# Context transposes spread between the first gate blocks of the odd layer, and the third block put ahead of the first context blocks

## The chip, the core and the metric

The kernel runs on one core of a Trainium2 chip. TensorE (PE), VectorE (DVE), ScalarE (ACT), GpSimd (POOL) and the DMA queues, most of them fed by SyncE (SP), run side by side and meet at semaphores. The metric is the device time of one execution, in microseconds.

## The reference

One step of a small diffusion backbone with two layers, on 1024 latent tokens and 256 context tokens of width 1024. The even layer is a gated attention with two kinds of heads. The odd layer, in which the change lies, mixes the tokens by a Fourier transform:

```python
def odd_mix(h, w_in, w_out):
    u, gate = jnp.split(h @ w_in, 2, axis=-1)
    return (fourier_mix(u) * jax.nn.silu(gate)) @ w_out
```

Here `h` is the normalised input after shift and scale, once for the latent and once for the context rows, which are treated as separate sequences. `fourier_mix` is the real part of a two-dimensional FFT over the positions and over 256 channels of each of four groups. All of it is in float32. Outputs are the two normalised token arrays and the even layer's keys and values of the context.

## The kernel before, in words

All products are made from split numbers: each float32 operand becomes a high part (rounded) and a low part (the rest), and a product is three matmuls, high by high, high by low, low by high (`mm3`, line 265). The even layer is attention over 128-query blocks and fills the first 700 us or so. Its output projection (`out_proj`, accumulators named `oz`) takes the ten 128-row blocks of tokens in pairs; blocks 8 and 9 are the context and come last.

Each finished row block is squared and summed (L1344); each pair is normalised and folded into a sum and a difference (L1356 to L1358, `xo_`, `xe`), which makes even and odd parts for the Fourier transform. Four latent folds make the eight rows called quads. The quads are transposed on TensorE into PSUM (`quad_T`, L1274; banks `eoE0` to `eoE7` for the even part, `eoO0` to `eoO7` for the odd) and evacuated with shift and scale into the split tiles `EH["E"]` and `EH["O"]`. An evacuation with a shift (`eo_shifted`, L1256 to L1258) is two ACTIVATEs on ScalarE and a subtraction on VectorE, by way of a tile of the zone `h`; one without (`eo_scaled`, L1263 and L1264) is one ACTIVATE and one VectorE operation. The pair of the context goes the same way in `ctx_T` (L1293, banks `eoC0` to `eoC3`, tiles `EH["C"]`): each of its four calls makes four transposes into one bank, each followed by its evacuation. PSUM has three banks for transposes.

Then comes the gate. Its 1024 columns are eight column tiles, `ct` 0 to 7, and the weights `w_g1` are loaded 256 columns at a time, so that one load serves two tiles (`load_w`: four DMAs on SP's queue, L298, into raw tiles of zone `h`, and four splits, the high part by ScalarE, L277, the low part by GpSimd, L283). For each tile there is a main block for the latent rows, here m0 to m7: 24 matmuls of 512 columns from the even tiles (`g1E`) and 24 from the odd ones (`g1O`), evacuated by ScalarE and VectorE (L1473 to L1480), put through SiLU (L1453, L1454) and written to DRAM. And there is a context block, here p0 to p7: 24 matmuls of 256 columns (`g1c`). Between them stand eight steps (r0 to r7, `Rows.step`, L358 and L362) that sum up the rows of the adaptive-modulation weights for the layer's output gate on VectorE, each with a 512 KB load. After the gate comes the projection `u` with weights `wd`, the Fourier sums, and the output projection.

Memory in SBUF is handed out by hand from zones, in source order: `take` gives the buffer of a zone that was given back first, `drop` gives one back, and the new user waits for the last old one. `h` has nine buffers; the five zones in `BIG` have 43 together. PSUM accumulators of the gate come from a ring (`next_bank`) of four places: `g`, `s`, `a`, `s`, where `g` and `a` stand for one bank each and `s` for three.

The order of each engine's instructions is not the source's. A planner goes over the program when it is built: it takes, at each simulated time, the first in source order of the instructions that are ready by its own costs. So the source gives ranks and the order of buffers, and the planner fills gaps with what stands further down.

Of the kernel before, what the change touches and what calls it, by code (L numbers as in the profile page):

```python
# [59 lines left out]
AT_C, WO1 = (1, 1), ((0, 1, 2, 3), (), (4,), (5, 6), (7,))  # L60
PAIRS = ((0, 4), (2, 6), (3, 7), (1, 5), (8, 9))
FILL_C, NLATE = 2.9, 8
E_FQ, E_GD = "d", "d"
ORDER = "qa0 qa1 kb0 qb0 qb1 g0 g1 g2 g3"
FLATE = "f3"
# [74 lines left out]
def hybrid_step(ctx: ExitStack, tc: tile.TileContext, I, O):  # L140
# [40 lines left out]
    def next_bank(name):  # L181
        ring.rotate(-1)
        return bank(ring[-1], name)
# [102 lines left out]
    def load_w(src, width=256, tags="w", gap=None, lc=E_WL, each=None, later=None):  # L286
        out = []
        for kp in range(2):
            hi = take(tags, (P, 4, width), F32R)
            lo = take(tags, (P, 4, width), F32R)  # L290
            for j in range(2):
                r0 = (kp * 4 + j * 2) * P
                if width <= 256:
                    raw = take("h", (P, 2, width))
                else:
                    raw = take(("p", "pt", "q", "w"), (P, 2, width))
                if gap is None:
                    sp.dma_start(raw.a, src[r0 : r0 + 2 * P, :].rearrange("(j p) f -> p j f", p=P))  # L298
                else:
                    gap(raw, r0)  # L300
                if each is not None:
                    each(raw, kp * 4 + 2 * j)

                def fin(raw=raw, hi=hi[:, 2 * j : 2 * j + 2, :], lo=lo[:, 2 * j : 2 * j + 2, :]):
                    split(hi, lo, raw.a, XE["wh"], lc)
                    drop(raw)

                if later is None:
                    fin()
                else:  # L310
                    later.append(fin)
            out.append((hi, lo))
        return out
# [5 lines left out]
    def wk(w, k, c0, n):  # L319
        h, l = w[k // 4]  # L320
        return h[:, k % 4, c0 : c0 + n], l[:, k % 4, c0 : c0 + n]
# [962 lines left out]
    def ctx_T(rows, kq):  # L1284
        if kq == 0:
            EH["C"] = [(take(BIG, (P, 4, 256), F32R), take(BIG, (P, 4, 256), F32R)) for _ in range(2)]
        hh, hl = EH["C"][kq // 2]
        tp = t_bank(f"eoC{kq}")
        for j in range(2):
            k = 2 * kq + j  # L1290
            for n, row in enumerate(rows):
                c0 = j * 256 + n * P
                pe.transpose(tp[:, c0 : c0 + P], row[:, k * P : k * P + P], ident)  # L1293
                cols = slice(n * P, n * P + P)
                (eo_scaled if n else eo_shifted)(hh[:, k % 4, cols], hl[:, k % 4, cols], tp[:, c0 : c0 + P], k, 1)
        if kq == 3:
            drop(*rows)

    def eo_cols(key, k, c0, n):
        kper = 4 if key == "C" else 2  # L1300
        hh, hl = EH[key][k // kper]
        return hh[:, k % kper, c0 : c0 + n], hl[:, k % kper, c0 : c0 + n]

    gt0 = {}
    pairs = PAIRS
    kept = []
    half = {}
# [12 lines left out]
    def proj_step(i, j):  # L1320
        r = pairs[i][j]
        n = 2 * i + j
        v = r // 8
        if n == 4:
            for u in range(2):
                dve.tensor_scalar(mod2[:, :, u], modb[:, 1, :, u], (4.0, 2.0)[u], None, op0=ALU.mult)

        def between(h):
            for key, k in BETWEEN.get((n, h), ()):
                quad_T(key, k)  # L1330
            if (n, h) == (9, 1):
                for hw, lw in wout:
                    drop(hw, lw)
                for k in range(OPRE, 8):
                    quad_T("O", k)

        xr = out_proj("oz", r, ins.pop(r), wout, gt0[v], between)
        if n == 7:
            drop(gt0.pop(0))
        if r == 9:  # L1340
            drop(gt0.pop(1))
        yt = take("h", (P, D), BF16)
        sp.dma_start(x1d[r * P : (r + 1) * P, :], xr.a)
        act.activation(yt.a, xr.a, AF.Square, accum_out=ss1[:, r : r + 1])  # L1344
        drop(yt)
        kept.append(xr)
        if j == 0:
            return 0
        ssp = sm.tile([P, 4], F32, tag="ssq", name=f"ssp{i}")[:, 0:2]
        for jj, rr in enumerate(pairs[i]):  # L1350
            dve.tensor_copy(ssp[:, jj : jj + 1], ss1[:, rr : rr + 1])
        rs = rsqrt(f"r1{i}", ssp, 2, 1.0 / D, pw=PW1[i] == "1")
        xa, xb = kept
        kept.clear()
        xo_, xe = take(OB[0], (P, D)), take(OB[0], (P, D))
        act.activation(xo_.a, xb.a, AF.Copy, scale=rs[:, 1:2])  # L1356
        dve.scalar_tensor_tensor(out=xe.a, in0=xa.a, scalar=rs[:, 0:1], in1=xo_.a, op0=ALU.mult, op1=ALU.add)
        dve.scalar_tensor_tensor(out=xo_.a, in0=xa.a, scalar=rs[:, 0:1], in1=xo_.a, op0=ALU.mult, op1=ALU.subtract)  # L1358
        drop(xa, xb)
        if i == 4:  # L1360
            for kq in range(4):
                ctx_T((xe, xo_), kq)
            return 0
        half[pairs[i][0]] = xe, xo_
        if i % 2 == 0:
            return 0
        z = 0 in half
        (eh, oh), (el, ol) = half.pop(2 if z else 3), half.pop(0 if z else 1)
        ep = take(OB[0], (P, D))
        pick("fq", E_FQ).tensor_add(ep.a, el.a, eh.a)  # L1370
        pick("fq", E_FQ).tensor_sub(eh.a, el.a, eh.a)
        drop(el)
        op = take(OB[0], (P, D))
        pick("fq", E_FQ).tensor_add(op.a, ol.a, oh.a)
        if z:
            act.activation(op[0:1, :], oh[0:1, :], AF.Copy)
        pick("fq", E_FQ).tensor_sub(oh.a, ol.a, oh.a)
        if z:
            act.activation(oh[0:1, :], ol[0:1, :], AF.Copy)
        drop(ol)  # L1380
        quads[0 if z else 1] = (ep, eh, op, oh)
        return 0
# [61 lines left out]
    XE.update(XE3)  # L1444
    fl_.drain()

    wg = wgs[0]

    def silu4(d, n, scale):
        th = take(BIG, (P, n))
# [2 lines left out]
        drop(th)  # L1455

    r2 = Rows(1, 2, "ad12", BIG)
    for c in range(4):
        wn = load_w(I["w_g1"][:, 256 * c + 256 : 256 * c + 512], tags=BIG) if c < 3 else None
        todo = []  # L1460
        for c2 in range(2):
            ct = 2 * c + c2

            def main(ct=ct, c2=c2, wg=wg):
                ps = []
                for key in "EO":
                    ps.append(next_bank(f"g1{key}{ct}"))
                    mm3(ps[-1], [(*wk(wg, k, c2 * P, P), *eo_cols(key, k, 0, 512)) for k in range(8)])
                so = take("h", (P, 512))
                un = [take("h", (P, 512)) for _ in range(2)]  # L1470
                for e in range(2):
                    sl = so[:, e * 256 : e * 256 + 256]
                    act.activation(sl, ps[e][:, 256:512], AF.Copy)  # L1473
                    dve.tensor_add(un[e][:, 0:256], ps[e][:, 0:256], sl)
                    dve.tensor_sub(un[e][:, 256:512], ps[e][:, 0:256], sl)
                dve.tensor_scalar(un[1][:, 0:1], so[:, 256:257], 2.0, None, op0=ALU.mult)
                dve.tensor_scalar(un[1][:, 256:257], ps[1][:, 0:1], 2.0, None, op0=ALU.mult)
                d = take(BIG, (P, D))
                pick("gd", E_GD).tensor_add(d[:, 0:512], un[0].a, un[1].a)
                pick("gd", E_GD).tensor_sub(d[:, 512:1024], un[0].a, un[1].a)  # L1480
                drop(so, *un)
                silu4(d, D, 0.125)
                sp.dma_start(g1d[ct, :, 0:1024], d.a)
                drop(d)

            def part(ct=ct, c2=c2, wg=wg):
                ps = next_bank(f"g1c{ct}")[:, 0:256]
                mm3(ps, [(*wk(wg, k, c2 * P, P), *eo_cols("C", k, 0, 256)) for k in range(8)])
                so = take("h", (P, P))
                act.activation(so.a, ps[:, P:], AF.Copy)  # L1490
                d = take("h", (P, 256))
                dve.tensor_add(d[:, 0:P], ps[:, 0:P], so.a)
                dve.tensor_sub(d[:, P:], ps[:, 0:P], so.a)
                drop(so)
                silu4(d, 256, 0.25)
                sp.dma_start(g1d[ct, :, 1024:1280], d.a)
                drop(d)

            todo.append((main, part))
        todo[0][0]()  # L1500
        todo[1][0]()
        for k in ((), (0, 1, 2), (3, 4, 5), (6, 7))[c]:
            r2.step(k)
        todo[0][1]()
        todo[1][1]()
        drop_w(wg)
        wg = wn
    r2.finish("g")


# [457 lines left out]
```

## Time and profile before

| | us |
|---|---|
| median of 3 runs | 1191.62 |
| lowest and highest | 1185.96, 1196.26 |
| span of the profiled execution, first to last instruction | 1196.9 |

The page gives no other time for the profiled execution than its span. Over the span the granted TensorE clock was 0.990 of full speed on average. The DMA queues moved 168.81 MB, 141 GB/s on average. Lines of a timeline give start and duration in us, engine, line of the kernel, operation, output from inputs (zones or names of tiles, moving operand first for a matmul), shape, count, and in brackets the idle time before it with its releaser. Matmuls overlap in time, so that their pace is seen from start to start. Zones appear as names: `u`, `w`, `q`, `pt`, `p` and `h` are kinds of SBUF buffers.

### The profile page before, as it was taken

The numbers are of one execution on the slowest core, as the hardware profiler recorded it, in microseconds if no ns is written. First come the engines' busy times: TensorE is split into PE (matmuls) and PEld (weight loads), VectorE is DVE, ScalarE is ACT, GpSimd is POOL, SyncE is SP. The second block draws the span as 40 slices with busy tenths as digits, with TensorE's granted clock in tenths as the row PEclk, the third lists the DMA queues.
The fourth block names the chain that finished last, engine by engine and source line by source line (L and its number), as shares of the span: only waits on it lengthen the run. The fifth ranks groups of instructions, "written<-read, shape, count | busy, mean of one in ns | idle before, by whom it ended". The sixth has DMA issues, their size and how long they took to land.

```text
span 1196.9 us, 22002 instructions
## 1 busy us (share of the span) xinstructions
PE 1159.1 (97%) x8103; PEld 1037.9 (87%) x8103; DVE 834.5 (70%) x2006; ACT 577.1 (48%) x1159; POOL 286.0 (24%) x272
## 2 busy tenths in 40 slices
PE   8999999999999999999999989998999999999997
PEld 6788899999999998899888878886878888998886
DVE  2489778787777776678888867777755964367543
ACT  4442555555656655556676654532364225333211
POOL 2255644512222230011010035200212226200001
PEclk9999999999999999999999989998998999999999
DMA  9978512323532232444354477774214435364321
GB/s 327 365 257 272 160 59 69 89 77 113 148 89 78 76 95 84 100 120 116 83 148 105 131 223 203 232 224 160 85 45 136 147 115 167 109 186 150 141 105 54
DMA packets 130096, 168.81 MB, mean 141 GB/s; under 512 B 26298, under 2 KB 86454, under 8 KB 129988
## 3 DMA queue, kind: packets, MB, share of 16 engines
q1 hardware_dynamic: 127476, 158.74, 43.5%
q0 software_dynamic: 2368, 8.39, 2.3%
q8 instruction: 64, 1.05, 0.4%
q14 instruction: 44, 0.36, 0.1%
q10 hardware_dynamic: 144, 0.26, 0.1%
HBM read 123.19 MB, written 44.16 MB: 140 GB/s over the span
## 4 chain that ended last, share of the span: by engine, by line
PE 80%; DMA 9%; DVE 5%; ACT 2%; issue 2%; SPq 1%; POOL 1%; POOLq 0%; DVEq 0%; ACTq 0%
PE of L265 9%; PE q L265 8%; PE av L1051 8%; PE pt L1045 8%; PE ga L265 7%; PE sL L928 5%; PE u L265 5%; PE oz L265 4%; PE g1E L265 4%; PE g1O L265 4%; PE kv L265 3%; PE sC L928 2%; PE wa L559 2%; PE g1c L265 2%; DMA h<-i_w_out 2%
## 5 line engine op out<-in xcount | busy, mean ns | idle before, releaser
L277 ACT ACTIVATE pt<-pt 128x512 fp32r<-128x512 f32 (+1 forms) x265 | 146.8, 575 | 107.0 <-PE pt L1045 60.2
L1048 DVE TENSOR_TENSOR pt<-pt,pt 128x512 fp32r<-128x512 f32 (+1 forms) x264 | 170.8, 658 | 37.7 <-ACT pt L277 36.8
L1051 PE MATMUL av<-pt,u 128*128 128x256 f32 x1008 | 167.1, 289 | 0.7 <-ACT pt L277 0.7
L1045 PE MATMUL pt<-identr,p 128*128 128x128 f32 x1008 | 157.4, 273 | 1.1 <-ACT p L969 0.8
L265 PE MATMUL q<-w,u 128*128 128x256 f32 x960 | 143.9, 287 | 0.0
L1051 PEld LDWEIGHTS av<-pt,u 128*128 128x128 f32 x1008 | 138.9, 190 | 4.6 <-ACT pt L277 0.9
L265 PEld LDWEIGHTS q<-w,u 128*128 128x128 f32 x960 | 126.8, 188 | 4.9 <-issue 0.8
L1045 PEld LDWEIGHTS pt<-identr,p 128*128 128x128 f32 x1008 | 119.7, 141 | 8.0 <-ACT p L969 1.0
L969 ACT ACTIVATE p<-p,nm 128x1280 f32<-128x1280 f32 (+1 forms) x80 | 95.5, 1194 | 63.1 <-DVE p L962 62.8
L265 PE MATMUL ga<-u,w 128*128 128x512 f32 (+1 forms) x576 | 124.1, 360 | 0.8 <-DVE byp L1024 0.5
L265 PEld LDWEIGHTS ga<-u,w 128*128 128x128 f32 x576 | 93.6, 188 | 15.2 <-ACT pt L277 1.2
L283 POOL TENSOR_TENSOR w<-h,w 128x512 fp32r<-128x512 f32 x38 | 51.1, 1360 | 143.4 <-DVE w L279 115.0
L928 PE MATMUL sL<-u,q 128*128 128x512 f32 x256 | 82.4, 411 | 2.0 <-DMA q<-qd 2.0
L969 ACT ACTIVATE p<-p,NM 128x640 f32<-128x640 f32 (+2 forms) x80 | 59.2, 740 | 39.5 <-DVE p L962 39.4
L928 PE MATMUL sC<-u,q 128*128 128x256 f32 x320 | 61.8, 294 | 1.6 <-DMA q<-qd 1.0
L962 DVE TENSOR_SCALAR_CACHE_REDUCE p<-sL 128x512 f32<-128x512 f32 x64 | 43.9, 685 | 23.2 <-PE sL L928 14.2
L962 DVE TENSOR_SCALAR_CACHE_REDUCE p<-sL,nm 128x512 f32<-128x512 f32 x64 | 47.7, 745 | 13.7 <-PE sL L928 12.9
L265 PE MATMUL oz<-u,w 128*128 128x512 f32 x192 | 57.3, 403 | 0.0
L283 POOL TENSOR_TENSOR u<-h,u 128x512 fp32r<-128x512 f32 x16 | 20.6, 1293 | 138.0 <-ACT u L277 133.9
L928 PEld LDWEIGHTS sC<-u,q 128*128 128x128 f32 x320 | 48.8, 189 | 5.5 <-issue 1.1
L265 PE MATMUL oz<-u,u 128*128 128x512 f32 x160 | 48.7, 405 | 4.0 <-ACT u L277 2.5
L702 POOL TENSOR_TENSOR h<-h,rope 128x512 f32<-128x512 f32 (+1 forms) x18 | 21.9, 1214 | 126.4 <-ACT h L785 80.5
(728 smaller groups left out, 2569.8 us busy)
## 6 DMA issues: line engine op xcount, KB each, us to landing
q<-qd SPq DMA_DIRECT2D x80, 256.0 KB
h<-i_w_in SPq DMA_DIRECT2D x40, 256.0 KB
p<-i_ada_w SPq DMA_DIRECT2D x18, 512.0 KB
h<-i_w_out SPq DMA_DIRECT2D x32, 256.0 KB
pt<-i_ada_w SPq DMA_DIRECT2D x15, 512.0 KB
qd<-pt SPq DMA_DIRECT2D x20, 256.0 KB
q<-i_ada_w SPq DMA_DIRECT2D x9, 512.0 KB
qd<-q SPq DMA_DIRECT2D x18, 256.0 KB
```

What stands on the lines that cost most here:

```text
L265: pe.matmul(out, a, b, start=i == 0, stop=i == n - 1)
L277: act.activation(out, in_, AF.Copy)
L283: pick("lo" + lc, lc).tensor_sub(dst_l, src, dst_h)
L559: pe.matmul(acc[:, i * 256 : i * 256 + 256], wu[j][:, c0 : c0 + P], f[:, j, :], start=j == 0, stop=j == 1)
L702: pick("rope", XE["rope"]).tensor_mul(t1.rearrange("p t h (b c) -> p t (h b) c", b=2), y.rearrange("p t h (b c) -> p t (h b) c", b=2), cb)
L928: pe.matmul(ps, q_at(q, s, hc), keys, start=s == 0, stop=s == 1)
L962: dve.tensor_scalar(p[i][:, end[i] : end[i] + n], ps, sign, last[i], op0=ALU.mult, op1=ALU.min, accum_out=c)
L969: act.activation(p[i][:, 0 : end[i]], p[i][:, 0 : end[i]], AF.Exp, bias=last[i], scale=-1.0, accum_out=SU[:, t, hd + i, 0:1],)
L1045: pe.transpose(tp[:, jj * 256 + i * P : jj * 256 + i * P + P], p[i][:, off : off + P], ident)
L1048: dve.tensor_sub(pt[:, 1, 0:n], tp[:, 0:n], pt[:, 0, 0:n])
L1051: pe.matmul(acc, vv, pt[:, s, jj * 256 : jj * 256 + 256], start=c + jj + s == 0, stop=c + jj == nt - 1 and s == 1,)
```

## The change

The four `ctx_T` calls leave the end of the last projection step. That step now only keeps the two context rows in a list. The gate's main block makes one call after each of its two accumulations for the first two column tiles: the first after m0's even part, the second after m0's odd part, the third and the fourth after those of m1. The nested loop over weights and column tiles becomes a list of operations, in which l is a load of weights, m a main block, p a context block, r a step of `Rows`, and d the giving back of weights. In the same notation the order was and is:

```
before: l1 m0 m1 p0 p1 d0  l2 m2 m3 r0 r1 r2 p2 p3 d1  l3 m4 m5 r3 r4 r5 p4 p5 d2  m6 m7 r6 r7 p6 p7 d3
after:  l1 m0 m1 m2 p0 p1 d0  l2 r0 r1 r2 m3 p2 p3 d1  l3 r3 r4 r5 m4 m5 p4 p5 d2  r6 r7 m6 m7 p6 p7 d3
```

Thus m2 stands ahead of p0 and p1, and each group of r steps stands ahead of the main blocks that it followed. Before, all of `ctx_T` stood ahead of l1; now it stands behind it.

```diff
+G1 = "l1 m0 m1 m2 p0 p1 d0 l2 r0 r1 r2 m3 p2 p3 d1 l3 r3 r4 r5 m4 m5 p4 p5 d2 r6 r7 m6 m7 p6 p7 d3"
...
+    ctx_rows = []
...
         if i == 4:
-            for kq in range(4):
-                ctx_T((xe, xo_), kq)
+            ctx_rows.extend((xe, xo_))
             return 0
...
-    for c in range(4):
-        wn = load_w(I["w_g1"][:, 256 * c + 256 : 256 * c + 512], tags=BIG) if c < 3 else None
...
-        todo[0][0]()
-        todo[1][0]()
-        for k in ((), (0, 1, 2), (3, 4, 5), (6, 7))[c]:
-            r2.step(k)
-        todo[0][1]()
-        todo[1][1]()
-        drop_w(wg)
-        wg = wn
+    WG = {0: wgs[0]}
+
+    def g1_main(ct):
+        w, c2 = WG[ct // 2], ct % 2
+        ps = []
+        for n, key in enumerate("EO"):
+            ps.append(next_bank(f"g1{key}{ct}"))
+            mm3(ps[-1], [(*wk(w, k, c2 * P, P), *eo_cols(key, k, 0, 512)) for k in range(8)])
+            if 2 * ct + n < 4:
+                ctx_T(ctx_rows, 2 * ct + n)
...
+    for op in G1.split():
+        nm, i = op[0], int(op[1:])
+        if nm == "l":
+            WG[i] = load_w(I["w_g1"][:, 256 * i : 256 * i + 256], tags=BIG)
+        elif nm == "m":
+            g1_main(i)
+        elif nm == "p":
+            g1_part(i)
+        elif nm == "r":
+            r2.step(i)
+        else:
+            drop_w(WG.pop(i))
     r2.finish("g")
```

The evacuation, the SiLU and the write of a main block and the whole of a context block (`g1_part`) are as they were.

More of the change, by code (lines that the diff above doesn't have):

```diff
@@ L1445, in hybrid_step @@
     fl_.drain()
-    wg = wgs[0]
     def silu4(d, n, scale):
@@ L1457, in hybrid_step @@
     r2 = Rows(1, 2, "ad12", BIG)
-    for c in range(4):
-        wn = load_w(I["w_g1"][:, 256 * c + 256 : 256 * c + 512], tags=BIG) if c < 3 else None
[L1460 to L1499, printed above, removed]
-        todo[0][0]()
-        todo[1][0]()
-        for k in ((), (0, 1, 2), (3, 4, 5), (6, 7))[c]:
-            r2.step(k)
-        todo[0][1]()
-        todo[1][1]()
-        drop_w(wg)
-        wg = wn
@@ new lines, in hybrid_step @@
+    WG = {0: wgs[0]}
[7 more added lines that the diff above has]
+                ctx_T(ctx_rows, 2 * ct + n)
+        so = take("h", (P, 512))
+        un = [take("h", (P, 512)) for _ in range(2)]
+        for e in range(2):
+            sl = so[:, e * 256 : e * 256 + 256]
+            act.activation(sl, ps[e][:, 256:512], AF.Copy)
+            dve.tensor_add(un[e][:, 0:256], ps[e][:, 0:256], sl)
+            dve.tensor_sub(un[e][:, 256:512], ps[e][:, 0:256], sl)
+        dve.tensor_scalar(un[1][:, 0:1], so[:, 256:257], 2.0, None, op0=ALU.mult)
+        dve.tensor_scalar(un[1][:, 256:257], ps[1][:, 0:1], 2.0, None, op0=ALU.mult)
+        d = take(BIG, (P, D))
+        pick("gd", E_GD).tensor_add(d[:, 0:512], un[0].a, un[1].a)
+        pick("gd", E_GD).tensor_sub(d[:, 512:1024], un[0].a, un[1].a)
+        drop(so, *un)
+        silu4(d, D, 0.125)
+        sp.dma_start(g1d[ct, :, 0:1024], d.a)
+        drop(d)
@@ new lines, in g1_part @@
+    def g1_part(ct):
+        w, c2 = WG[ct // 2], ct % 2
+        ps = next_bank(f"g1c{ct}")[:, 0:256]
+        mm3(ps, [(*wk(w, k, c2 * P, P), *eo_cols("C", k, 0, 256)) for k in range(8)])
+        so = take("h", (P, P))
+        act.activation(so.a, ps[:, P:], AF.Copy)
+        d = take("h", (P, 256))
+        dve.tensor_add(d[:, 0:P], ps[:, 0:P], so.a)
+        dve.tensor_sub(d[:, P:], ps[:, 0:P], so.a)
+        drop(so)
+        silu4(d, 256, 0.25)
+        sp.dma_start(g1d[ct, :, 1024:1280], d.a)
+        drop(d)
```

## The prediction

> **What bounds the kernel now.** I read the page first, for the engine that carries the end.
>
> ```profile
> span 1196.9 us, 22002 instructions
> ...
> PE 1159.1 (97%) x8103; PEld 1037.9 (87%) x8103; DVE 834.5 (70%) x2006; ACT 577.1 (48%) x1159; POOL 286.0 (24%) x272
> ...
> PE 80%; DMA 9%; DVE 5%; ACT 2%; issue 2%; SPq 1%; POOL 1%; POOLq 0%; DVEq 0%; ACTq 0%
> ```
>
> TensorE is busy 97% of the span and carries 80% of the chain that ended last. So a change pays only where PE stands idle or runs slowly. The second view is busy time by stretches of time, cut around the stage that the change touches (columns: stretch and length, busy time and instructions of PE, PEld, DVE, ACT, POOL, granted clock, DMA share, GB/s).
>
> ```profile
> 838.00:894.95 56.95, 56.95 (x281) 46.51 (x280) 38.04 (x60) 28.52 (x53) 9.40 (x9) 1.00 0.18 62
> 894.95:906.77 11.82, 9.57 (x49) 8.23 (x48) 8.23 (x25) 8.91 (x24) 3.84 (x3) 0.71 0.19 59
> 906.77:1190.00 283.23, 283.23 (x1705) 245.19 (x1703) 165.72 (x329) 84.39 (x180) 54.04 (x52) 1.00 0.42 135
> ```
>
> PE has no idle time from 838 to 894.95 and none from 906.77 to the end, both at clock 1.00. Between them lies one bad stretch of 11.82 us: 2.25 us idle (11.82 - 9.57), clock 0.71. Nothing behind it can swallow a gain made there, because PE is full for the 283 us that follow; nothing behind it can add to one either. The third view is PE's order of instructions around that stretch.
>
> ```profile
> 894.72 0.39 PE L265 MATMUL g1O<-u,u 128*128 128x512 f32 x1
> 894.95 0.49 PE L1293 MATMUL eoC<-identr,u 128*128 128x128 f32 x3
> 896.29 0.38 PE L265 MATMUL g1c<-u,u 128*128 128x256 f32 x1 [0.85 <-ACT u L1263]
> 898.32 0.33 PE L1293 MATMUL eoC<-identr,u 128*128 128x128 f32 x1 [0.79 <-ACT h L1257]
> 899.01 0.47 PE L1293 MATMUL eoC<-identr,u 128*128 128x128 f32 x1 [0.37 <-ACT h L1257]
> 906.77 0.40 PE L265 MATMUL g1O<-p,u 128*128 128x512 f32 x1
> ```
>
> Main work (g1O) ends at 894.95; then PE has only context transposes (eoC) and context blocks (g1c) that need those transposes, and waits for ScalarE's evacuations. Main work resumes at 906.77. How much main work was done before the hole is the row of g1E alone: 48 matmuls, two blocks of 24, so m0 and m1.
>
> ```profile
> 866.00:895.00 29.00, 13.29 (x48) 8.43 (x48) 0.00 (x0) 0.00 (x0) 1.00 0.11 38
> ```
>
> The work at 906.77 is thus the third and fourth blocks. Why did it not come earlier? Its weights (l1) were late: SP's issues, SP's waits, and ScalarE's splits (L277) of those loads say so.
>
> ```profile
> 871.20 0.40 SPq L298 DMA_DIRECT2D h<-i_w_g  x1
> 892.35 0.38 SPq L298 DMA_DIRECT2D h<-i_w_g  x1
> 899.09 0.37 SPq L298 DMA_DIRECT2D h<-i_w_g  x1
> ...
> SPq L298 <- DVE u L1258: 26.8, 3, 20.7
> ...
> 874.74 0.63 ACT L277 ACTIVATE u<-h 128x512 fp32r<-128x512 f32 x1
> 895.35 0.63 ACT L277 ACTIVATE u<-h 128x512 fp32r<-128x512 f32 x1 [0.33 <-DMA h<-i_w_g]
> 901.72 0.63 ACT L277 ACTIVATE u<-h 128x512 fp32r<-128x512 f32 x1 [0.74 <-DMA h<-i_w_g]
> ```
>
> The first of l1's four loads is issued at 871.20 and split at 874.74. The others wait, 20.7 us the longest, for VectorE's L1258, the subtraction that ends the use of an `h` tile by a context transpose's evacuation. The last is split at 901.72. The nine `h` buffers are handed out in source order, and in the source the eight `h` tiles of the context transposes stand ahead of l1's raw tiles.
>
> **The change part by part.** *What can be won.* The stretch of 11.82 us holds this PE work:
>
> ```profile
> 894.95:906.77 11.82, 7.67 (x36) 7.14 (x36) 0.00 (x0) 0.00 (x0) 0.71 0.19 59
> 894.95:906.77 11.82, 3.27 (x11) 1.50 (x10) 1.82 (x6) 5.22 (x16) 0.71 0.19 59
> 930.63:936.29 5.66, 5.66 (x48) 5.61 (x47) 0.00 (x0) 0.28 (x1) 1.00 0.54 164
> ...
> 867.74 0.27 PE L1274 MATMUL eoE<-identr,p 128*128 128x128 f32 x1
> 867.85 0.27 PE L1274 MATMUL eoE<-identr,u 128*128 128x128 f32 x1
> ```
>
> The first row is g1c alone (36 matmuls), the second eoC alone (11 transposes), the third g1c alone where nothing disturbs it: 48 in 5.66 us, a pitch of 0.118 us. A transpose undisturbed has a pitch of 0.11 us (867.74 to 867.85). At full pace the stretch is 36 x 0.118 + 11 x 0.11 = 5.46 us, so it loses 11.82 - 5.46 = **6.36 us**. Its parts: 2.25 us idle; the clock; and 1.70 us left over, matmuls and transposes that come singly and are shown at their own length instead of their pitch. The clock part is seen in two stretches:
>
> ```profile
> 894.95:899.97 5.02, 2.77 (x13) 1.53 (x12) 2.43 (x8) 4.50 (x14) 2.56 (x2) 0.88 0.17 51
> 899.97:905.55 5.58, 5.58 (x27) 5.48 (x27) 4.85 (x16) 3.46 (x10) 1.28 (x1) 0.50 0.14 47
> ```
>
> In 5.58 us at clock 0.50 PE does 27 instructions (25 g1c, 2 eoC) that take 3.17 us at full pace: 2.41 us lost. No row gives the clock gate's rule, only that 2.77 us of work in 5.02 us was followed by half speed. The Trainium skill, "TensorE: Matmul & The Clock Gate", Part 1, puts the fall to half clock down to idle gaps of more than about 3 us, and its Part 4 adds that transposes do not count as PE work in the same way. The longest idle shown here is 0.85 us, so the trace differs from the first as stated and fits the second; by the gap rule alone the dip would not belong to this stall, and the sum would lose its 2.41 us.
>
> *Transposes spread, third main block ahead.* The number of matmuls and transposes is unchanged. What moves is source rank: l1's loads now stand ahead of all context evacuations, so their raw tiles follow the eoE evacuations and the last row's square; I expect all four issued and split before about 885 (issue to split took 3.5 us at 871.20, and nothing that they would follow is left after the last eoE evacuation). m2's two accumulations then stand ready when m1 ends. They cover the hole:
>
> ```profile
> 918.81 1.55 PE L265 MATMUL g1E<-w,u 128*128 128x512 f32 x6
> 920.20 1.09 PE L265 MATMUL g1E<-u,u 128*128 128x512 f32 x4
> ```
>
> Six matmuls in 920.20 - 918.81 = 1.39 us are 0.232 us each, so m2's 48 give 11.1 us of PE work, and the 16 transposes can be evacuated beside it and beside m0 and m1 instead of being waited for one by one. The context blocks p0 and p1 (5.66 us) then run where PE now runs m2. The cover's price if it fails is the hole as it is now.
>
> *A new order of waiting.* p0 and p1 are now behind m2 on PE; if l1 is late, 5.66 us of ready work waits behind m2, and with it the release of wg0 (d0) and l2's loads. Bank by bank nothing new is needed: m2's E bank is the one of m0's E, whose evacuation stood in the present order behind the same `h` tiles as l1 and moves forward with them. The two context rows stay in their buffers some 15 us longer, and the context tiles are taken after l1's; weights, E, O, context, accumulators and rows are 32 of 43 large buffers by the code, so nothing waits for one. I count all this at zero; the cover is m2's 11.1 us.
>
> *Row steps r0 to r2 ahead of m3 (and r3 to r7 likewise).* No step is added.
>
> ```profile
> 915.02 2.74 DVE L362 SCALAR_TENSOR_TENSOR u<-u,cs,u 128x512 f32<-128x512 f32 x4 [1.93 <-DMA u<-i_ada_w]
> ```
>
> Three steps are 3 x 2.74 = 8.2 us of VectorE ahead of m3's evacuation, and three 512 KB loads that SP issues earlier, behind l2's four, ahead of the blocks' output writes. The bank that m4's E needs is m3's E, free only once VectorE has read it; between the two PE has m3's O (5.6 us) and p2, p3 (5.7 us), 11.2 us against 8.2 and 1.9 of wait. Tight but covered: zero. Were it not, PE would wait for the difference.
>
> *The splits of l1 in the eoE/eoO evacuation.* This is the price. Three splits that now lie at 895 to 902 move to where ScalarE and VectorE feed PE's transposes: 3 x 0.63 = 1.9 us of ScalarE, each with a wait for its DMA (0.33 and 0.74 above; the longest near by is the first row here), and three subtractions on POOL.
>
> ```profile
> 908.61 0.63 ACT L277 ACTIVATE p<-h 128x512 fp32r<-128x512 f32 x1 [2.10 <-DMA h<-i_w_g]
> ...
> 873.62 1.28 DVE L1357 SCALAR_TENSOR_TENSOR u<-u,r14y,u 128x1024 f32<-128x1024 f32 x1 [0.66 <-ACT u L1356]
> 875.55 2.27 DVE L1358 SCALAR_TENSOR_TENSOR u<-u,r14y,u 128x1024 f32<-128x1024 f32 x1
> ...
> 875.45 1.29 POOL L283 TENSOR_TENSOR u<-h,u 128x512 fp32r<-128x512 f32 x1 [3.05 <-ACT u L277]
> ```
>
> While POOL made the one subtraction that is already there, a VectorE operation of the same size took 2.27 us and not 1.28: 0.99 us more. The Trainium skill, "SBUF — State Buffer", section "Who interferes with whom", states that a VectorE instruction with two SBUF inputs contends with a GpSimd instruction that reads SBUF; the trace agrees (2.27 against 1.28), and by that rule it speaks against this change, which moves three more such subtractions (up to 3.0 us of VectorE) there. From above, the cost is 3 x (0.63 + 2.10) = 8.2 us on ScalarE's queue, all of it reaching PE; from below it is zero, because the split at 874.74 with its subtraction cost PE nothing (no idle from 838 to 894.95). A gain is excluded: PE has no idle there. I take 0.3 us for each, 0.9 us, near the row of 874.74.
>
> *Sum.* -6.36 + 0.9 = -5.5 us. The page gives no time of the profiled execution besides its span: 1196.9 us, 0.6 above the slowest of the three runs (1196.26) and 5.3 above their median. The difference goes onto the median: 1191.6 - 5.5 = **1186 us** (1191.4 as a span). A measurement of this kernel can tell about 1% from no change, 12 us, and the whole hole is 6.4 us: 0.5%.
>
> **The rivals.**
>
> *The change doesn't do what it says.* The order on the engines isn't the source's: m3's O runs beside m2's O, and context matmuls run ahead of m2. A planner with costs of its own fills gaps; it can again release the context transposes as soon as a bank is free and leave PE with singles, or place l1 late. For it: in the present order it put them at 894.95 to 900 though they starved PE. Against it: it did so with no other main block ready. It gives back 0 to 2 us: 1190 to 1191.6.
>
> *Slower: a new hole in the transposes' stage.* Place: 866 to 890, ScalarE in order behind l1's DMA waits, VectorE stretched by POOL. Price: up to the 8.2 us above, plus a half-clock stretch of 2.4, less the 6.36 gained: +4.2, so 1196. It decides against the change once PE's new idle time passes about 4 us (4 + 2.4 = 6.4). That a hole of some us brings the clock down is seen twice, that 1.6 us did not, once:
>
> ```profile
> 690.00:700.00 10.00, 5.49 (x36) 4.94 (x35) 2.76 (x9) 3.35 (x9) 3.09 (x6) 0.87 0.73 241
> 730.00:740.00 10.00, 8.40 (x49) 7.18 (x48) 9.96 (x20) 4.36 (x11) 5.67 (x3) 1.00 0.35 119
> 810.00:820.00 10.00, 5.57 (x24) 3.94 (x23) 8.47 (x10) 3.02 (x6) 0.31 (x1) 0.84 0.60 174
> ```
>
> Against it: ScalarE has only 28.52 us of work in the 56.95 us before the hole, VectorE 38.04.
>
> *The half clock is not this hole's.* If the dip comes from something else and stays, the gain is 6.36 - 2.41 - 0.9 = 3.1 us: 1188.6. Against it: clock 1.00 in every stretch behind it, and 0.50 right after it.
>
> *The order elsewhere shifts.* A rebuilt plan may move things behind 907, where PE has nothing to gain, or ahead of 866, where 4.4 us (10 - 5.57) are idle in the stretch from 810 alone. No part of the diff points there; either sign, some us, 1180 to 1197.
>
> **How the numbers follow.** Forecast 0.54 (its own range 1182 to 1190: cost 0 to 3 us, and the runs' spread of 1185.96 to 1196.26 around a median of three); dip stays 0.04; no effect 0.20; new hole 0.12; order elsewhere 0.10. The range leaves out half of the last case and the far end of the slower one: 1180 to 1195. Faster by over 1% (below 1179.7) needs more than the hole holds, so it comes from the last case and the runs' spread: 0.08. Slower by over 1% (above 1203.5) needs a new hole worth more than priced: 0.06. Within 1%: 0.86.
>
> **What would show it.** Right: from 866 to the end PE without idle and at clock 1.00; 72 g1E matmuls ahead of the first g1c; eoC transposes apart from each other with main matmuls between; l1's four SP issues before 880. Wrong: idle time in eoE/eoO with a ScalarE or VectorE releaser; L277 waiting for `i_w_g` there; eoC still one by one with waits; PE waiting at m4 for a bank. The prediction fails as a whole if l1's loads stay behind another `h` user, or if what PE gains in this stage comes back as a new stop behind 907.

## The result: 0.5% slower, and the profile after

The changed kernel takes 1199.42 us against 1192.56 us before (medians of 17 runs each). The ratio is 1.0053, with a 95% interval of 1.0037 to 1.0068: 6.3 us slower (0.0053 x 1192.56), where 5.5 us faster was forecast. One run of the changed kernel took 2920.82 us and is left out of the ratio. The profiled execution of the changed kernel took 1196.54 us, its span is 1194.7.

The page of the changed kernel: span, busy time of PE, shares of the chain that ended last.

```profile
span 1194.7 us, 22000 instructions
...
PE 1158.0 (97%) x8103; PEld 1037.7 (87%) x8103; DVE 835.8 (70%) x2006; ACT 578.4 (48%) x1159; POOL 292.5 (24%) x272
...
PE 80%; DMA 9%; DVE 6%; issue 2%; ACT 2%; POOL 1%; SPq 1%; POOLq 0%; DVEq 0%; ACTq 0%
```

Nothing is to be seen at that scale, and this span is even shorter than the first one of before. The two executions differ most ahead of the change: the first gate product starts at 858.5 here and at 866.6 there. The 8 us are there before the change acts: up to l1's first load, at 853.20 here, every engine's instructions stand in the same order in both. So from here on I compare only the stretch from the first gate product (`g1E`) to the last product of the output projection (`of`), and call it **the stretch**. It took 329.1 us here and 323.2 in the profile of before. Busy time by stretches of time in the changed kernel (columns as in the prediction):

```profile
858.50:871.64 13.14, 11.65 (x63) 9.30 (x61) 9.73 (x15) 10.83 (x22) 6.75 (x5) 1.00 0.31 100
871.64:921.60 49.96, 49.32 (x267) 41.26 (x268) 29.75 (x63) 21.73 (x46) 8.10 (x4) 1.00 0.28 92
921.60:925.92 4.32, 0.52 (x5) 0.34 (x4) 3.28 (x8) 0.84 (x4) 0.00 (x0) 0.75 0.93 333
925.92:930.94 5.02, 5.02 (x24) 5.02 (x25) 5.02 (x14) 1.79 (x5) 0.00 (x0) 0.53 0.37 108
930.94:986.80 55.86, 55.86 (x290) 47.33 (x288) 39.84 (x75) 14.32 (x28) 14.30 (x10) 1.00 0.22 81
986.80:996.10 9.30, 7.37 (x76) 4.34 (x75) 3.00 (x4) 4.79 (x10) 6.81 (x6) 0.97 0.93 265
```

The old hole is gone: 49.96 us from 871.64 with 0.64 us idle and clock 1.00. In its place stand three new losses. PE's timeline names the releaser of each:

```profile
871.64 0.33 PE L1275 MATMUL eoO<-identr,pt 128*128 128x128 f32 x1 [1.49 <-DVE pt L1265]
...
925.92 5.18 PE L266 MATMUL g1c<-u,u 128*128 128x256 f32 x24 [3.80 <-DVE h L1491]
...
994.84 0.43 PE L1546 MATMUL xr<-q,e 128*32 128x130 f32 x8 [1.33 <-DMA q<-wd]
```

**The big one** is the second. PE waits 3.80 us for the bank of the context block that runs fourth (by the ring of banks it is p2, which takes p0's place); behind the wait 24 matmuls take 5.02 us at clock 0.53, where at the pitch of 0.118 us they take 24 x 0.118 = 2.83: 2.2 us more. ScalarE and VectorE in those microseconds:

```profile
921.75 0.75 ACT L1488 ACTIVATE h<-g1c 128x128 f32<-128x128 f32 x3 [1.04 <-PE g1c L266]
```

```profile
922.64 2.74 DVE L363 SCALAR_TENSOR_TENSOR u<-u,cs,u 128x512 f32<-128x512 f32 x4 [1.35 <-DMA u<-i_ada_w]
925.30 0.28 DVE L1490 TENSOR_TENSOR h<-g1c,h 128x128 f32<-128x128 f32 x1
925.50 0.28 DVE L1491 TENSOR_TENSOR h<-g1c,h 128x128 f32<-128x128 f32 x1
```

ScalarE has copied its half of the three context banks by 922.50. VectorE, which must read the other half (L1490, L1491) before a bank is free, stands at that time in a Rows step (L363; it is r1, since r0 ran at 903.69): first 1.35 us for the step's load, then 2.74 us for its four operations. The reads come after it, and PE goes on 0.14 us after the first L1491 has ended.

### The profile page after: what moved, and what is told of

Same layout as the page of the kernel before. It is cut to its first block, busy times and chain, and to the rows that moved or that the text cites. A ratio compares the mean times of both kernels' runs of the same rounds, so it can differ in the third digit from the quotient of the medians.

```text
span 1194.7 us, 22000 instructions
## 1 busy us (share of the span) xinstructions
PE 1158.0 (97%) x8103; PEld 1037.7 (87%) x8103; DVE 835.8 (70%) x2006; ACT 578.4 (48%) x1159; POOL 292.5 (24%) x272
## 4 chain that ended last, share of the span: by engine, by line
PE 80%; DMA 9%; DVE 6%; issue 2%; ACT 2%; POOL 1%; SPq 1%; POOLq 0%; DVEq 0%; ACTq 0%
PE of L266 9%; PE av L1052 9%; PE ga L266 8%; PE pt L1046 8%; PE q L266 8%; PE oz L266 5%; PE sL L929 5%; PE u L266 5%; PE g1O L266 4%; PE g1E L266 3%; PE kv L266 3%; PE sC L929 3%; PE g1c L266 2%; PE sB L1001 1%; DMA q<-qd 1%
## 5 line engine op out<-in xcount | busy, mean ns | idle before, releaser
L266 PE MATMUL of<-u,u 128*128 128x512 f32 (+1 forms) x187 | 58.0, 388 | 0.0
```

The source lines that it names most:

```text
L266: pe.matmul(out, a, b, start=i == 0, stop=i == n - 1)
```

## The experiments

Ratios are to the kernel before, those of the experiments with 12 runs each; b1 to b3 and a1 are one execution each and stand in the first two rows. The table has the stretch and its parts, in us; the gate is from the first `g1E` to the last `g1c`, the u stage from there to the first product of the Fourier sums. Idle time is that of PE. Each experiment has one profile, and four profiles of before differ by 2.0 us in the stretch: a smaller difference between two rows says something only where a named wait goes with it.

| kernel | gate | idle, clock | u stage | idle | stretch | ratio [95%] |
|---|---|---|---|---|---|---|
| before, four profiles | 125.4, 123.5, 124.9, 124.0 | 2.2, 2.6, 1.8, 1.9 | 69.6 to 69.7 | 0 | 323.2, 321.2, 322.7, 321.7 | 1 |
| after, two profiles | 128.2, 128.5 | 5.9 and 6.0, 0.97 | 72.6, 70.8 | 1.9, 1.6 | 329.1, 327.6 | 1.0053 [1.0037, 1.0068] |
| e1, steps back | 122.3 | 2.5, 1.00 | 70.6 | 0 | 321.2 | 0.9995 [0.9975, 1.0014] |
| e2, spread only | 125.5 | 4.3, 1.00 | 69.6 | 0 | 323.4 | 1.0024 [1.0001, 1.0047] |
| e3, m2 only | 122.7 | 1.9, 1.00 | 70.4 | 0 | 321.4 | 1.0001 [0.9980, 1.0023] |
| e4, steps only | 130.3 | 6.7, 0.97 | 69.4 | 0 | 327.8 | 1.0063 [1.0040, 1.0087] |
| f1, early loads | 123.7 | 3.1, 1.00 | 72.1 | 1.7 | 324.2 | 1.0016 [0.9991, 1.0041] |
| f2, r0 to r2 ahead | 128.3 | 6.0, 0.97 | 70.6 | 0 | 327.2 | 1.0045 [1.0025, 1.0065] |
| f3, r3 to r7 ahead | 122.3 | 2.6, 1.00 | 72.5 | 1.8 | 323.0 | 1.0011 [0.9992, 1.0031] |
| f4, l1's low parts on VectorE | 120.7 | 1.0, 1.00 | 70.6 | 0 | 319.6 | 0.9989 [0.9965, 1.0013] |
| h4, the same again | 120.9 | 1.0, 1.00 | 70.5 | 0 | 319.8 | 0.9995 [0.9975, 1.0015] |
| h1, bank by ScalarE | 122.3 | 2.3, 1.00 | 71.3 | 2.3 | 321.9 | 1.0014 [0.9994, 1.0034] |
| h2, m2 and l1 on VectorE | 124.9 | 2.8, 0.99 | 70.4 | 0 | 323.6 | 1.0028 [1.0007, 1.0048] |
| h3, all three | 120.8 | 0.7, 1.00 | 70.3 | 0 | 319.4 | 0.9997 [0.9980, 1.0015] |

### Which part of the change costs

The change has three parts: contexts spread, m2 ahead, r steps ahead. **e1** takes the steps back, **e2** and **e3** keep one of the other parts alone, **e4** keeps the steps alone (`early` stands for the four `ctx_T` calls put back at the end of the projection).

```diff
 # e1
-G1 = "l1 m0 m1 m2 p0 p1 d0 l2 r0 r1 r2 m3 p2 p3 d1 l3 r3 r4 r5 m4 m5 p4 p5 d2 r6 r7 m6 m7 p6 p7 d3"
+G1 = "l1 m0 m1 m2 p0 p1 d0 l2 m3 r0 r1 r2 p2 p3 d1 l3 m4 m5 r3 r4 r5 p4 p5 d2 m6 m7 r6 r7 p6 p7 d3"
 # e2: the order of before
+G1 = "l1 m0 m1 p0 p1 d0 l2 m2 m3 r0 r1 r2 p2 p3 d1 l3 m4 m5 r3 r4 r5 p4 p5 d2 m6 m7 r6 r7 p6 p7 d3"
 # e3: e1's order, early
 # e4: early, and
+G1 = "l1 m0 m1 p0 p1 d0 l2 r0 r1 r2 m2 m3 p2 p3 d1 l3 r3 r4 r5 m4 m5 p4 p5 d2 r6 r7 m6 m7 p6 p7 d3"
```

> The changed kernel with its r steps put back behind the main blocks (r0 to r2 behind m3, r3 to r5 behind m5, r6 and r7 behind m7); transposes spread and m2 ahead as in the change. Theory A (the r steps stand ahead of evacuations on VectorE, one of them waits for its load, and so a context block waits for its PSUM bank): the hole of 3.8 us at the context blocks and its half clock are gone, about 1191 to 1192, the 6.4 us of the old hole gained and some 1.5 us in the eoO stage and 3 us at the wd loads still lost. Theory B (the context blocks are bunched because the spread transposes finish late; the r steps are innocent): the hole stays, 1198 to 1200.

> The kernel before with one part of the change: the context transposes spread between m0 and m1; m2 stays behind the context blocks, the r steps where they were. Theory A: the old hole is filled because l1 comes early, no new one, about 1187 to 1189. Theory B: the late transposes leave PE waiting at the context blocks, 1192 or more. Both expect a VectorE wait of about 1.5 us in the eoO stage, where l1's low parts on GpSimd now run.

> The kernel before with one part of the change: m2 put ahead of p0 and p1; the transposes stay at the end of the last projection step. l1's raw tiles still follow the context evacuations in the h zone. If l1's lateness makes the old hole, it stays: 1191 to 1194. If only the rank of m2 behind the context blocks makes it, it is filled: 1186 to 1188.

> The kernel before with one part of the change: the r steps put ahead of the main blocks that they followed; transposes and m2 as before. Theory A: a new hole at m3 to m4 or at p2, p3, 1196 to 1200. Theory B: no new hole, 1191 to 1194.

With the steps back the loss is gone (0.9995); with the steps alone it is there in full (1.0063), in a kernel whose contexts are neither spread nor behind m2. PE's wait at the place of the hole, in e1 and then in e4:

```profile
927.12 3.06 PE L266 MATMUL g1c<-u,u 128*128 128x256 f32 x24 [0.57 <-DVE h L1491]
```

```profile
925.58 2.90 PE L266 MATMUL g1E<-w,u 128*128 128x512 f32 x6 [4.01 <-DVE h L1490]
```

3.80 us has become 0.57 in e1. In e4 it is 4.01, and the fourth block of even products waits there (72 `g1E` matmuls, three blocks, stand before it); by the ring it is m3's E, in p0's place. The victim changes, the releaser on VectorE is again a context block's read behind Rows steps.

Spread alone and m2 alone bring no gain that the times show: e3 stands at 1.0001, and e2 missed its gain of 2 to 4 us (1.0024, interval just above 1). In e2 l1 comes early and the planner runs m2 ahead of p0 and p1 by itself: 72 `g1E` and 96 `g1O` matmuls stand before 913.7. But m3's even products need p0's bank and wait 0.75 us for its read by VectorE (L1491), beside 1.0 and 0.8 us of waits for the context evacuations and 1.6 us at `eoO`: 4.3 us idle in all. In e3 the last of l1's splits still begins only at 901.34, and 1.9 us stay idle.

### Which steps, and is it their place on VectorE

**f2** and **f3** put one group of steps ahead each, on top of e1. **f1** leaves the change's order and issues the three loads of r0 to r2 right behind l1's.

```diff
 # f2
+G1 = "l1 m0 m1 m2 p0 p1 d0 l2 r0 r1 r2 m3 p2 p3 d1 l3 m4 m5 r3 r4 r5 p4 p5 d2 m6 m7 r6 r7 p6 p7 d3"
 # f3
+G1 = "l1 m0 m1 m2 p0 p1 d0 l2 m3 r0 r1 r2 p2 p3 d1 l3 r3 r4 r5 m4 m5 p4 p5 d2 r6 r7 m6 m7 p6 p7 d3"
 # f1
+G1 = "l1 w0 w1 w2 m0 m1 m2 p0 p1 d0 l2 r0 r1 r2 m3 p2 p3 d1 l3 r3 r4 r5 m4 m5 p4 p5 d2 r6 r7 m6 m7 p6 p7 d3"
+        elif nm == "w":
+            WT[i] = take(BIG, (P, D))
+            sp.dma_start(WT[i].a, ada_src(1, 2, i))
 ...
```

> The changed kernel with r3 to r7 put back behind their main blocks; r0 to r2 stay ahead of m3. If r0 to r2 alone make the hole of 3.8 us and its half clock, and r3 to r7 the loss of some 3 us at the wd loads: the hole stays and the wd stall goes, 1194 to 1196 against 1191 of before.

> The changed kernel with r0 to r2 put back behind m3; r3 to r7 stay ahead. By the same reading the hole at the context blocks goes and the wd stall (PE waits about 2 us for wd, then runs at a reduced clock) stays: 1193 to 1195. If r3 to r7 cost nothing: 1190 to 1191, as with all of them put back.

> The changed kernel, with the 512 KB loads of r0, r1 and r2 issued right behind l1 instead of in the steps themselves; the VectorE work of the three steps keeps its place in the list. Theory A1 (what hurts is that a step in VectorE's queue waits for a late load, with the evacuations behind it): the hole at the context blocks goes, about 5 to 6 us faster than the changed kernel, 1192 to 1194 against 1191 of before. Theory A2 (it is the 8.2 us of VectorE work ahead of the evacuations): the hole stays, 1197 or more.

The hole belongs to r0 to r2 and the stall in the u stage to r3 to r7. In f2 PE waits 3.85 us at the same place, and the u stage has no idle time; in f3 it is the other way round. Taken against e1 the two add up: 327.2 - 321.2 = 6.0 and 323.0 - 321.2 = 1.8 make 7.8, and the changed kernel stands 7.9 and 6.4 above e1 in its two profiles. The times show the first of the two costs (f2 1.0045) but not the second (f3 1.0011, interval from 0.9992).

Most of the 1.8 us goes with half clock. Behind the wait for `wd` the granted clock is 0.50 for about 3.4 us in f3 (994.4 to 997.8), f1 (from 993.2) and the first profile of the changed kernel (from 995.5), and their u stage takes 72.5, 72.1 and 72.6 us. In the second profile and in h1 the wait is shorter (0.86 and 0.83 us against 1.25 to 1.54) and the clock stays at 1.00: 70.8 and 71.3, against 70.6 in e1.

PE's timeline of f2:

```profile
929.46 5.28 PE L266 MATMUL g1c<-u,u 128*128 128x256 f32 x24 [3.85 <-DVE h L1491]
```

f1 did not test quite what it was made for. With the loads issued from 861.24 the planner also ran the steps themselves early: all twelve operations of r0 to r2 lie between 864.98 and 878.47, and the context blocks' reads come from 926.72 with no step just ahead of them (the step at 931.17 is r3). So it shows that the hole goes when no step stands ahead of the reads (PE waits 0.58), and says nothing of what an earlier load would do for a step that keeps its place on VectorE.

**h1** is the direct test: steps, order and loads as in the change, but a context block's bank is emptied by ScalarE alone, so that its release does not pass through VectorE.

```diff
-        so = take("h", (P, P))
-        act.activation(so.a, ps[:, P:], AF.Copy)
+        so = take("h", (P, 256))
+        act.activation(so.a, ps, AF.Copy)
         d = take("h", (P, 256))
-        dve.tensor_add(d[:, 0:P], ps[:, 0:P], so.a)
-        dve.tensor_sub(d[:, P:], ps[:, 0:P], so.a)
+        dve.tensor_add(d[:, 0:P], so[:, 0:P], so[:, P:])
+        dve.tensor_sub(d[:, P:], so[:, 0:P], so[:, P:])
```

> The changed kernel, with one edit: each context block's bank is emptied by ScalarE alone (it copies all 256 columns into SBUF, VectorE then adds and subtracts there), so that the bank's release no longer stands in VectorE's queue behind Rows steps; the steps stay where the change put them. Theory (the hole is the release stuck behind the steps on VectorE): the wait of 3.80 us before the fourth context block's products at 925.92 falls under 0.6, the half-clock stretch behind it goes (2.35 us), the gate's stretch is 122 to 123 against 128.2, and the time falls by about 5 us, ratio to before near 1.001; the wd stall of about 2 us in the u stage stays. Rival (the hole is the late transposes or the context blocks' place, and VectorE's queue only accompanies it): the hole and the low clock stay, 128 us, ratio 1.005.

VectorE's timeline of h1 at the same place (all times lie 8 us later in this execution), then PE's:

```profile
930.79 2.74 DVE L363 SCALAR_TENSOR_TENSOR u<-u,cs,u 128x512 f32<-128x512 f32 x4 [1.27 <-DMA u<-i_ada_w]
933.45 0.28 DVE L1490 TENSOR_TENSOR h<-h 128x128 f32<-128x128 f32 x1
```

```profile
929.83 3.67 PE L266 MATMUL g1c<-u,u 128*128 128x256 f32 x27
933.34 0.39 PE L266 MATMUL g1O<-p,w 128*128 128x512 f32 x1
```

VectorE does the same in the same order, with a wait of 1.27 us for the load (1.35 in the changed kernel) and the same step of 2.74 us ahead of the context blocks' additions. PE runs through it without a wait and at clock 1.00. The gate is 122.3 us, as in e1, and the ratio falls from 1.0053 to 1.0014. The stall in the u stage stays, as expected. So **the hole is shown to be the bank's release standing in VectorE's queue behind a step and its load**. Neither the late transposes nor the place of the context blocks makes it; both are as in the change here.

### The wait of eoO: GpSimd's subtractions

**f4** is e1 with the low parts of l1's weights made by VectorE instead of GpSimd; **h4** is the same kernel once more, **h2** makes this edit on e3, **h3** adds it and h1's edit to e1.

```diff
-            WG[i] = load_w(I["w_g1"][:, 256 * i : 256 * i + 256], tags=BIG)
+            WG[i] = load_w(I["w_g1"][:, 256 * i : 256 * i + 256], tags=BIG, lc="d" if i == 1 else E_WL)
```

> The changed kernel with all r steps put back behind the main blocks, and with the low parts of l1 subtracted on VectorE instead of GpSimd. If GpSimd's subtractions stretch VectorE's in the eoE stage and so make PE wait 1.5 us at eoO, the wait goes or shrinks to under 0.5 us and VectorE's operations there fall back to their usual 0.42 and 1.28 us: 1 to 1.5 us faster than with GpSimd, 1188 to 1189. If it is the work as such, VectorE has 2.7 us more of it and the wait grows: 1190 to 1192.

> The same kernel as f4_l1_low_dve, beside the others of this call: spread and third main block ahead, Rows steps as before, l1's low parts on VectorE. If its gain of 3.6 us in the profiled stage is real, the ratio is 0.997 (1188 to 1189 against 1191 to 1193); if the stage gain does not reach the end, 1.000.

> The third main block ahead of the first context blocks, transposes and Rows steps as before the change, and the low parts of l1's weights on VectorE rather than GpSimd. If the l1 splits' GpSimd work is what takes the 1.5 us wait of eoO for VectorE: that wait is gone, and the stretch from the first g1E to the end is 2 to 4 us under before's 323.2 (the m2-only kernel: 321.4), ratio 0.996 to 0.999. If the splits cost nothing that PE sees: as the m2-only kernel, ratio 1.000.

> Transposes spread and the third main block ahead, as in the change; Rows steps as before it; l1's low parts on VectorE; context banks emptied by ScalarE alone. If every hole found is a release in VectorE's queue: no wait over 0.6 us of PE in the gate, clock 1.00, the gate 119.5 to 120.7 against 125.4 before, ratio 0.995 to 0.998. If the bank's release no longer matters once the steps are back: as the kernel without this last edit, gate 120.7, ratio 0.999.

VectorE in the changed kernel while GpSimd subtracts, GpSimd there (e1 has the same picture), then VectorE in f4:

```profile
867.56 2.19 DVE L1360 SCALAR_TENSOR_TENSOR u<-u,r14y,u 128x1024 f32<-128x1024 f32 x1
869.67 1.52 DVE L1259 TENSOR_TENSOR pt<-h,u 128x256 fp32r<-128x256 f32 x1
```

```profile
866.70 4.21 POOL L284 TENSOR_TENSOR u<-h,u 128x512 fp32r<-128x512 f32 x2 [0.26 <-ACT u L278]
```

```profile
869.92 0.68 DVE L284 TENSOR_TENSOR u<-h,u 128x512 fp32r<-128x512 f32 x1
870.52 1.28 DVE L1360 SCALAR_TENSOR_TENSOR u<-u,r14y,u 128x1024 f32<-128x1024 f32 x1
871.72 0.42 DVE L1259 TENSOR_TENSOR pt<-h,u 128x256 fp32r<-128x256 f32 x1
```

Two VectorE operations lose 0.91 and 1.10 us beside GpSimd. Without it they take 1.28 and 0.42, and the subtraction that VectorE does in GpSimd's stead costs 0.68. The wait of 1.49 us before `eoO` is gone, the gate falls by 1.6 us (122.3 to 120.7; 120.9 in h4). h2 missed: where the contexts are not spread, l1's splits do not lie there. It has three of them from 892.32 on, in the old hole, so nothing was to be won there, and more is lost in the old hole than in e3 (2.8 us idle against 1.9, clock 0.99, gate 124.9). Its ratio of 1.0028 lies above 1, more than its stretch explains. That also shows what moves l1: with the contexts spread, its first split in e1, e2 and the changed kernel begins at 856.94 to 861.79 and its last at 867.78 to 872.67; without, in e3 and h2, the last begins at 901.34 and 898.86.

The gate of h3 as one row, then that of e1:

```profile
863.50:984.30 120.80, 120.11 (x645) 101.11 (x644) 87.15 (x174) 50.49 (x104) 21.28 (x16) 1.00 0.32 105
```

```profile
863.40:985.70 122.30, 119.78 (x645) 100.95 (x643) 86.39 (x171) 49.75 (x104) 26.44 (x20) 1.00 0.31 104
```

h3 has 0.69 us without a matmul (120.80 - 120.11), no wait over 0.5 us, and the shortest stretch of all. Its expected ratio of 0.995 to 0.998 was missed all the same. No version is measurably faster than before; f4, h4 and h3 stand at 0.9989, 0.9995 and 0.9997, so that of h4's two expectations "does not reach the end" came out.

### Is the old hole's half clock there every time

> The kernel before, unchanged: a second profile of it. The first one holds 323.2 us from the first gate product to the last output product, with 2.24 us without a matmul and 2.41 us of half clock in the hole at 894.95 to 906.77. If the half clock belongs to every execution: 323 us again, granted clock 0.97 in the gate's stretch. If it comes and goes: 320.5 to 321.5 us, the idle time in place, clock 0.99 to 1.00, and the gain that a filled hole can bring is that much smaller.

> As the run before it, a third profile of the kernel before: 323 us with a clock of 0.97 in the gate's stretch if the half clock is of every execution, 320.5 to 321.5 us with 0.99 to 1.00 if it isn't.

> A fourth profile of the kernel before, read as the two ahead of it: 323 us and 0.97, or 320.5 to 321.5 us and 0.99 to 1.00.

> The changed kernel, unchanged: a second profile of it. If its own hole (3.80 us of waiting and 2.35 us of half clock behind it) belongs to every execution: 328 to 330 us from the first gate product to the last output product, clock 0.97. If the half clock comes and goes here too: about 326.5 us with the wait in place.

The 11.82 us of the old hole, in the three new profiles of before, at the same distance from the first `g1E`; then the gate of the changed kernel in its second profile:

```profile
889.45:901.27 11.82, 9.79 (x60) 7.92 (x59) 8.68 (x25) 8.77 (x24) 3.86 (x3) 1.00 0.22 72
```

```profile
885.95:897.77 11.82, 10.01 (x51) 8.58 (x50) 8.76 (x25) 8.85 (x24) 3.83 (x3) 0.71 0.20 66
```

```profile
890.75:902.57 11.82, 9.88 (x55) 8.29 (x54) 8.71 (x25) 8.85 (x24) 3.83 (x3) 0.86 0.20 68
```

```profile
857.10:985.60 128.50, 122.51 (x645) 103.45 (x643) 86.52 (x171) 49.53 (x103) 28.30 (x19) 0.97 0.28 97
```

The idle time is there each time (2.03, 1.81 and 1.94 us, against 2.25 in the first). The half clock comes and goes: clock 0.71 in the first profile, then 1.00, 0.71 and 0.86, with 49, 60, 51 and 55 instructions done in the same 11.82 us. The stretch of before is 322.2 us on the mean of four, not 323.2. The changed kernel's hole has both times the wait of 3.8 us and the half clock. On the means, 328.35 - 322.2 = 6.15 us, which is what the times say (6.3).

## Why the prediction was wrong, point by point

**The step that failed** is "Row steps r0 to r2 ahead of m3 (and r3 to r7 likewise) ... Tight but covered: zero." It priced one bank, that of m4's E. It did not ask which other reads stand behind the steps on VectorE at the time when the planner lets them run: those of the three context blocks that ran first, whose banks the next blocks need. m2 put ahead of p0 and p1 brought the context blocks to just that place, but e4 shows that the steps hit a bank without that too. Measured: 6.0 us for r0 to r2 (f2 against e1: 3.85 us of waiting where e1 has 0.57, and the half clock behind it), 1.8 us for r3 to r7 (f3 against e1, most of it a half clock that not every execution has). Its own fallback, "Were it not, PE would wait for the difference", was the right mechanism at another bank; and it left out the half clock behind the wait.

**"Nothing behind it can swallow a gain made there ... nothing behind it can add to one either"** failed with it. A stage in which PE has no idle time is full in the old order; a change of order makes its own holes in it. The prediction's last line named this outcome, "a new stop behind 907", but gave it no price.

**The old hole, -6.36 us.** That it could be filled, and by what, was right: idle 0.64 us from 871.64 to 921.60. The size was too large. f4 and h4, where the new waits are away, have a stretch of 319.6 and 319.8 against 322.2: 2.5 us won. In the gate alone it is 3.65 us (120.8 against 124.45 on the means); 0.9 us of it goes again in the u stage (70.55 against 69.65), without idle time there, and why stays open. Of the prediction's terms, the 2.41 us of half clock were those of one execution; of four profiles of before one has none of it.

**The rule on the clock.** The prediction noted that the half clock came with a longest idle gap of 0.85 us. Both kinds of hole are now in the rows: 3.80, 3.78, 3.85 and 4.01 us of waiting (after twice, f2, e4) each went with a clock of 0.97 in the gate; 0.85 us and less did in some executions of before and not in others, before the `xr` products, which need `wd`, 1.25, 1.33 and 1.54 us did (f3, after, f1) while 0.83 and 0.86 did not (h1, after again), and 1.49 to 1.64 us at `eoO` never did.

The Trainium skill, "TensorE: Matmul & The Clock Gate", section "What's actually happening", says that activity is judged over a free-running window of about 3.4 us. The traces agree: in all 18 the granted clock holds for whole multiples of 3.41 us ahead of its last record, and half clock lasted 3.41 or 6.83 us each time, but for the spell that the end of the span cuts off (in the changed kernel it is 0.50 from 923.8 to 930.6 and 1.00 on both sides). This raster lies differently against the stage in each execution: in the four of before an edge comes 28.8, 27.9, 28.4 and 29.4 us behind the first `g1E`, where the old hole begins at 28.35, and the hole had 6.83, 0, 6.83 and 3.41 us of half clock. That the place of the raster decides it is likely but not shown, and neither is how little work in a window brings the clock down.

**l1's loads ahead** was right. SP's issues in the changed kernel, then the last of ScalarE's splits of l1:

```profile
853.20 0.38 SPq L299 DMA_DIRECT2D h<-i_w_g  x1
...
860.88 3.96 SPq L299 DMA_DIRECT2D h<-i_w_g  x3
```

```profile
867.78 0.63 ACT L278 ACTIVATE u<-h 128x512 fp32r<-128x512 f32 x1
```

All four are issued by 864.84 and split by 868.41, where before the last split began at 901.72.

**The splits' price, 0.9 us**, had the right mechanism and was too low: PE waits 1.49 us, and taking GpSimd out of it gives 1.5 us (321.2 to 319.7 on the mean of f4 and h4). It went by the one split that had cost nothing; three together did not fit under the same cover. The Trainium skill, "SBUF — State Buffer", section "Who interferes with whom", says that a VectorE instruction with two SBUF inputs contends with a GpSimd instruction that reads SBUF. It is borne out by f4: 2.19 and 1.52 us become 1.28 and 0.42.

**The sum of the measured terms**: -2.5 + 1.5 + 6.0 + 1.8 = +6.8 us, against +6.9 and +5.4 in the stretch of the two profiles (the second has no half clock in the u stage) and +6.3 in the times. The prediction took 1% for the least that a measurement can tell; here 0.5% came out clear of its interval.

**The rivals.** The slower one came nearest in price (+4.2 us) and had the shape (over 4 us of new idle time and a half-clock stretch), but the wrong place and mechanism, so that its nearness is luck: it put the hole into the transposes' stage at 866 to 890, where 1.49 us were lost; the 3.80 us came at 922, at a bank. "What would show it" named PE waiting at m4 for a bank; it was a context block. "The half clock is not this hole's" was partly so.

**What stays open.** Why r3 to r7 ahead delay `wd`. In the changed kernel the first pair of `wd` loads is issued at 962.95 and the next at 985.49, in before six are issued from 951.91 to 966; but e4, with the same steps ahead and the contexts as before, has no such stall (four issued from 966.02 to 972.53), nor has f2 (four from 952.09). In all of them the next pair waits until a context block's products are done (9.8 us of waiting in the changed kernel), so what differs is how many loads get in before that wait: two with the stall, four or six without. Order on SP's queue and order of buffers were not told apart. Also open: the times of the twelve other kernels stand 1.3 us on the mean (-0.1 to 2.4) higher than their stretch against 322.2 says (h3: -0.4 us by the times, -2.8 by the stretch). That lies within or near each interval, but on one side.

## What to carry to other kernels

Before long work is moved ahead on an in-order engine, list every accumulator bank that this engine has still to release behind it, in the order in which the engine will really run, and charge each with the work and with its wait for data; here 1.35 + 2.74 us of VectorE became 3.80 us of PE and 2.2 us of half clock. If the work must stand there, let another engine empty the banks: one wider copy on ScalarE gave the 3.9 thousandths back. And profile the kernel before more than once before a gain is counted on a loss, such as a dip of the clock, that may belong to one execution.

## What was not expected of the hardware

The same program with the same stall ran at half clock for part of the old hole in three of four executions and at full clock in the fourth, and a spell of half clock came only in lengths of 3.41 and 6.83 us. The start of the gate moved by 9 us between executions of the same program ahead of it (857.6 to 866.6 in the four profiles of before), while the stretch behind it moved by 2.0: single spans would have ranked the changed kernel ahead.
